# Weight sums built by DMA in DRAM: 128 small steps over all of a layer in place of 64 larger steps inside its attention loop

## The chip, the cores and the metric

The kernel runs on one core of one Trainium2 chip. The metric is the device time of one execution in microseconds. Of the kernel before, three runs gave 1980.7, 1981.05 and 1982.59 us; the median, 1981.05 us, is the figure that the changed kernel is compared with.

## The reference

Two layers of a decoder trunk, for one sequence of 512 tokens and 1024 channels in float32. Cut to what matters here:

```python
for layer in range(2):
    z = rmsnorm(x) @ w_in[layer]                    # one wide projection, split into the mixers' inputs
    # three mixers: conformer convolution, sparse attention, latent attention
    x = x + (g_conv * y_conv + g_attn * y_nsa + g_mla * y_mla) @ w_out[layer]
    x = x + memory_cross_attention(rmsnorm(x), rmsnorm(mem), w_xq, w_xkv, w_xo)
    gate, up = split(rmsnorm(x) @ w_gate_up[layer])  # w_gate_up: 1024 x 5632, gate | up
    x = x + (silu(gate) * up) @ w_down[layer]
return rmsnorm(x)
```

The feed-forward product with `w_gate_up` is done with a scheme that multiplies fewer blocks than the plain product and needs, beside the weights, four sums of weight blocks. With g and u for the gate and up halves and 1 and 2 for the upper and lower 512 rows, the kernel puts together `u1+u2`, `g1+u1+u2`, `g1+u1` and `g1+g2+u1+u2` by signs that it arranges elsewhere; each is 512 rows by 2560 columns.

## The kernel before, in words

Every weight arrives by a load on SP's queue into a tile `raw` of 1 MB (two buffers), is split by `hilo` (L90 to L98) into a high part (ScalarE, L94) and a low remainder (VectorE, L95), and is used in three products per block, `mm3` (L84 to L87). TensorE is the engine with the most work. A layer passes, in order, through: the norm of x and its transposes; the projections with the convolution and the compression work (the loads `in_cmp_w_...` belong to it); the attention loop at the end of `mix`; the products with `w_out` (`residual`); cross attention; its `residual`; the feed-forward with the sums; the `residual` with `w_down`.

The four sums of a layer, `sums[0]` to `sums[3]`, are built in DRAM by DMAs alone: a plain DMA copies a block of weights into a sum, an accumulating DMA adds another block to it, and the last two steps of a job add one sum to another. `summed` (L330) makes a generator of these steps. A job is eight steps on one block of 320 columns and all 512 rows (row pieces of 1280 bytes, 640 KB a step): four copies, then four additions; eight jobs make 64 steps a layer. The attention loop calls `next(paced, None)` once per turn (L1099), which issues one step. Only POOL's queue can issue these steps, in order, and each waits for three things where they apply: the newest product of `mm3` at the time it was written (`latest["product"]`, a semaphore of TensorE, so that steps are paced), the step that wrote the sum it reads or adds to, and the DMA that used its completion semaphore before.

POOL has little else to do, but what it has stands in the same queue: the power -1/2 of every norm (`rs`, L202, in `rstd_of`; `mv`, L772, in the layer norm of the convolution; `rst`, L1032), for which VectorE waits before it can go on, and small memsets (`Pc`, `PTh`, `xt`, `u`). The feed-forward loads the sums column block by column block (two of 256 columns by 512 rows at a time, `ub` and `uc` in the last loop over m).

The order of instructions on each engine is made by a scheduler from the order of the code and its own estimates, so a step written between two products may land a few instructions away.

Of the kernel before, what the change touches and what calls it, by code (L numbers as in the profile page):

```python
# [3 lines left out]

# [9 lines left out]
OP = mybir.AluOpType  # L14
# [15 lines left out]
FFN = 2816  # L30
# [21 lines left out]
def kernel(ctx, tc, x, mem, positions, rel_bias, norm_mix, norm_xattn, norm_mem, norm_ffn, norm_final,  # L52
# [31 lines left out]
    def mm3(o, lh, ll, rh, rl, start, stop):  # L84
        nc.tensor.matmul(o, lh, rh, start=start, stop=False)  # L85
        nc.tensor.matmul(o, lh, rl, start=False, stop=False)  # L86
        latest["product"] = nc.tensor.matmul(o, ll, rh, start=False, stop=stop)  # L87

    latest = {}

    def hilo(hi, lo, src, scale=None):

# [97 lines left out]
    def load_gain(vec):  # L190
        g = new("gB", (128, D))
        nc.scalar.dma_start(g, rows_bcast(vec, D))
        return g
# [136 lines left out]
    def summed(l):  # L330

        W = w_gate_up[l]
        n, step = FFN - 256, 320
        sums = [dr.tile([512, n], F32, name=f"sums{l}_{i}") for i in range(4)]
        quarter = [(0, FFN), (0, 0), (0, 0), (512, 0)]
        jobs = []
        for c in range(0, n, step):
            s = [t[:, c:c + step] for t in sums]  # L340
            w = [[W[r:r + 512, o + 256 + c:o + 256 + c + step] for r in (0, 512)] for o in (0, FFN)]
            jobs.append([(s[0], w[1][0], None), (s[2], w[0][0], None), (s[1], w[0][0], None), (s[3], w[0][1], None),
                         (s[0], w[1][1], OP.add), (s[2], w[1][0], OP.add), (s[1], s[0], OP.add), (s[3], s[1], OP.add)])

        def steps():
            for job in jobs:
                for dst, src, op in job:
                    yield
                    d = nc.gpsimd.dma_start(dst, src, accum_op=op) if op else nc.gpsimd.dma_start(dst, src)  # L349

                    tc.add_manual_dep(d.ins, latest["product"].ins.name, mybir.DependencyInfo(
                        mybir.DependencyClass.Sync, mybir.DependencyReason.DATA), reason="paced")

        return sums, steps()

    def mix(l, x_src, g_mix, x_now, more_x, paced):
        W = w_in[l]


# [732 lines left out]
        for u, (_, mix, args) in enumerate(units):  # L1092
            scores = start(u + 2 if u < 3 else u + 3)
            for now in mix(*args, ready[u]):
                next(scores, None)
                products()
                products = now
                pump(6 if u < 4 else 4 if args[1] > 1 else 3)
                next(paced, None)  # L1099
            for _ in scores:  # L1100
                pump(1)
        products()
# [15 lines left out]
    def residual(acts, kt, w, xs, after, tail=2):  # L1118

        tags = ("t", "t", "s", "s", "mm", "mm", "mm", "pv")  # L1120
        accs = [bank(tag) for tag in tags]
        held = []

        def tokens(a, t):

            if len(a.shape) == 3:
                return a[:, t // 2, t % 2 * 128:(t % 2 + 1) * 128]
            return a[:, t * 128:(t + 1) * 128]

        def run(group, t):  # L1130
            for c in range(2):
                for k, wh, wl in group:
                    xh, xl = (tokens(a, t) for a in acts(k))
                    o = accs[2 * t + c]
                    r = slice(c * 512, (c + 1) * 512)
                    nc.tensor.matmul(o, xh, wh[:, r], start=k == 0, stop=False)  # L1136
                    nc.tensor.matmul(o, xh, wl[:, r], start=False, stop=False)  # L1137
                    nc.tensor.matmul(o, xl, wh[:, r], start=False, stop=k == kt - 1)  # L1138

        for u in row_units(w, kt):  # L1140
            held.append(u)
            if len(held) > tail:
                g = [held.pop(0)]
                for t in range(NT):
                    run(g, t)
        for t in range(NT):
            run(held, t)
            for c in range(2):
                nc.vector.tensor_tensor(xs[t][c], xs[t][c], accs[2 * t + c], op=OP.add)
            after(t)  # L1150
# [12 lines left out]
    x_src = xin  # L1163
    g_mix = load_gain(norm_mix[0])
    xs = load_x(xin, [], (0,))
    for l in range(L):
        sums, paced = summed(l)
        fin = mix(l, x_src, g_mix, lambda t: xs[t], lambda: l or load_x(xin, xs, (1, 2, 3)), paced)
        xs = load_x(x_src, [])


# [121 lines left out]


        last = l == L - 1
        g_next = load_gain(norm_final if last else norm_mix[l + 1])
        act = []
        homes = ["op"] * 10 + ["ca"] * 2 + ["PT"] * 2 + ["gm", "h", "h", "u"] + ["o8"] * 2 + ["BT"] * 2
# [129 lines left out]

        xs = load_x(xd, [])
        if not last:  # L1430
            def after(t):
                for c in range(2):
                    nc.scalar.dma_start(xd[t * 128:(t + 1) * 128, c * 512:(c + 1) * 512], xs[t][c])
        else:
            def after(t):
                for c, h in enumerate(norm_rows(xs[t], g_next)):
                    nc.sync.dma_start(out[0, t * 128:(t + 1) * 128, c * 512:(c + 1) * 512], h)
# [56 lines left out]
```

## Time and profile before

| | |
|---|---|
| runs, us | 1980.7, 1981.05, 1982.59 |
| profiled execution: its own time | 1980.79 us |
| its span (first to last instruction) | 1979.0 us |
| mean granted TensorE clock | 0.991 of 2.4 GHz |
| TensorE busy | 1929.8 us (98%) |
| VectorE, ScalarE, POOL busy | 69%, 50%, 8% |
| DMA moved | 317.92 MB, mean 161 GB/s |
| of it on POOL's queue (the steps, and 16 stores of x) | 88.09 MB, 20.6% of 16 engines' span |

The profiled execution took 1.8 us more than its span, which lies around the first and last instruction. In the page's slices the DMA engines are over 0.8 busy only in two stretches, 134 to 440 us and 1108 to 1425 us of the span: there the 64 steps of a layer are issued. Elsewhere they are at 0.2 to 0.6. A busy TensorE is not one at its peak, since the ends of matmuls are modelled; idle time in front of its instructions is what the waits show.

### The profile page before, as it was taken

How to read it: one execution, taken by the hardware profiler on the slowest of the kernel's cores; microseconds unless marked ns; L12 is line 12 of the kernel's file. 1: busy time of each engine (PE TensorE's matmuls, PEld its weight loads, DVE VectorE, ACT ScalarE, POOL GpSimd, SP SyncE). 2: the span in 40 equal slices, each digit the busy share in tenths (PEclk: the TensorE clock that was granted, in tenths of full speed). 3: DMA queues.
4: the chain of work that ended last, by engine and by line, in shares of the span. 5: the costliest groups of instructions: out<-in, count | busy, mean ns of one | idle time of the engine just before them, and what ended most of it. 6: DMA issues, size and time to landing. Idle time of an engine off the chain costs nothing.

```text
span 1979.0 us, 28842 instructions
## 1 busy us (share of the span) xinstructions
PE 1929.8 (98%) x11136; PEld 1679.1 (85%) x11136; DVE 1373.4 (69%) x2525; ACT 980.3 (50%) x1858; POOL 157.2 (8%) x236
## 2 busy tenths in 40 slices
PE   8998998999999999999999989989999999999998
PEld 8877887888888999988888868868888889999886
DVE  6988898764466877752279889976644677777423
ACT  5366556763355545531254755666633465545312
POOL 0001122210001000000000011222100010000000
PEclk9999999999999999999999989999999999999999
DMA  5247999893432455553232588979933434556431
GB/s 163 72 142 186 236 213 231 207 231 110 148 117 103 153 182 190 171 193 107 93 110 78 168 221 203 227 196 210 229 115 117 139 117 158 184 176 196 161 107 64
DMA packets 241397, 317.92 MB, mean 161 GB/s; under 512 B 12480, under 2 KB 203203, under 8 KB 241260
## 3 DMA queue, kind: packets, MB, share of 16 engines
q1 hardware_dynamic: 194028, 220.83, 34.4%
q0 software_dynamic: 44288, 88.09, 20.6%
q10 hardware_dynamic: 2944, 7.17, 1.0%
q8 instruction: 87, 1.43, 0.3%
q14 instruction: 50, 0.41, 0.1%
HBM read 307.64 MB, written 92.30 MB: 202 GB/s over the span
## 4 chain that ended last, share of the span: by engine, by line
PE 78%; issue 7%; DMA 6%; DVE 5%; ACT 2%; POOL 1%; SPq 0%; DVEq 0%; POOLq 0%; ACTq 0%
PE ps_mm L85 12%; PE ps_mm L86 12%; PE ps_mm L87 12%; PE ps_s L85 2%; PE ps_s L86 2%; PE ps_s L87 2%; PE ps_t L85 2%; PE ps_t L86 2%; PE ps_t L87 2%; PE ps_mm L1136 2%; PE ps_mm L1138 2%; PE ps_mm L1137 2%; DMA raw<-in_cmp_w_v_dram 2%; PE ps_t L952 2%; PE ps_t L1136 1%
## 5 line engine op out<-in xcount | busy, mean ns | idle before, releaser
L95 DVE TENSOR_TENSOR wl<-raw,wh 128x1024 fp32r<-128x1024 f32 (+5 forms) x382 | 451.3, 1185 | 382.9 <-ACT wh L94 381.4
L94 ACT CAST wh<-raw 128x1024 fp32r<-128x1024 f32 (+5 forms) x382 | 387.9, 1019 | 580.1 <-PE ps_pv L1138 206.7
L85 PE MATMUL ps_mm<-hTh,wh 128*128 128x512 f32 (+1 forms) x1152 | 417.5, 363 | 0.5 <-DVE kc L95 0.5
L86 PE MATMUL ps_mm<-hTl,wh 128*128 128x512 f32 (+1 forms) x1152 | 413.0, 359 | 0.0
L87 PE MATMUL ps_mm<-hTh,wl 128*128 128x512 f32 (+1 forms) x1152 | 411.9, 358 | 0.5 <-DVE wl L95 0.5
L87 PEld LDWEIGHTS ps_mm<-hTh,wl 128*128 128x128 f32 x1152 | 218.9, 190 | 33.0 <-DVE wl L95 1.3
L85 PEld LDWEIGHTS ps_mm<-hTh,wh 128*128 128x128 f32 x1152 | 219.4, 191 | 31.1 <-issue 3.3
L86 PEld LDWEIGHTS ps_mm<-hTl,wh 128*128 128x128 f32 x1152 | 219.3, 190 | 26.5 <-issue 0.7
L456 DVE SCALAR_TENSOR_TENSOR ca<-u,vT,ca 128x512 f32<-128x512 f32 x240 | 177.4, 747 | 2.9
L349 POOL DMA_DIRECT2D sums<-in_w_gate_up_dram x96 | 78.4, 824 | 337.2 <-PE ps_mm L87 229.0
L94 ACT CAST PTh<-ps_t 128x512 fp32r<-128x512 f32 (+4 forms) x136 | 70.3, 517 | 67.8 <-PE ps_t L952 53.2
L916 ACT ACTIVATE P<-P,ss 128x512 f32<-128x512 f32 (+3 forms) x128 | 71.3, 558 | 58.9 <-DVE ss L913 58.1
L85 PE MATMUL ps_s<-rh,wh 128*128 128x256 f32 x320 | 90.6, 283 | 0.0
L86 PE MATMUL ps_s<-rl,wh 128*128 128x256 f32 x320 | 90.6, 283 | 0.0
L87 PE MATMUL ps_s<-rh,wl 128*128 128x256 f32 x320 | 90.6, 283 | 0.0
L95 DVE TENSOR_TENSOR PTl<-ps_t,PTh 128x512 fp32r<-128x512 f32 (+2 forms) x120 | 71.6, 597 | 8.6 <-ACT PTh L94 7.5
L924 ACT ACTIVATE P<-P,sr 128x512 f32<-128x512 f32 (+3 forms) x128 | 63.2, 553 | 17.0 <-DVE sr L922 16.8
L202 POOL TENSOR_TENSOR rs<-rs,mhalf 128x1 f32<-128x1 f32 x32 | 22.4, 699 | 600.8 <-DVE rs L199 589.3
L85 PE MATMUL ps_mm<-op,wh 128*128 128x512 f32 (+1 forms) x192 | 69.1, 360 | 0.0
L86 PE MATMUL ps_mm<-op,wh 128*128 128x512 f32 (+1 forms) x192 | 68.2, 355 | 0.0
L87 PE MATMUL ps_mm<-op,wl 128*128 128x512 f32 (+1 forms) x192 | 68.2, 355 | 0.0
L85 PEld LDWEIGHTS ps_s<-rh,wh 128*128 128x128 f32 x320 | 61.4, 192 | 0.0
(552 smaller groups left out, 4553.4 us busy)
## 6 DMA issues: line engine op xcount, KB each, us to landing
sums<-in_w_gate_up_dram POOLq DMA_DIRECT2D x96, 640.0 KB, 7.2
raw<-sums SPq DMA_DIRECT2D x80, 512.0 KB
raw<-in_w_in_dram SPq DMA_DIRECT2D x32, 1024.0 KB
raw<-in_w_gate_up_dram SPq DMA_DIRECT2D x24, 1024.0 KB
raw<-in_w_down_dram SPq DMA_DIRECT2D x22, 1024.0 KB
sums<-sums POOLq DMA_DIRECT2D x32, 640.0 KB, 7.5
raw<-in_w_in_dram SPq DMA_DIRECT2D x26, 512.0 KB
raw<-in_w_gate_up_dram SPq DMA_DIRECT2D x20, 512.0 KB
```

Of the source, the lines that this page charges most:

```text
L85: nc.tensor.matmul(o, lh, rh, start=start, stop=False)
L86: nc.tensor.matmul(o, lh, rl, start=False, stop=False)
L87: latest["product"] = nc.tensor.matmul(o, ll, rh, start=False, stop=stop)
L94: nc.scalar.copy(hi, src)
L95: nc.vector.tensor_tensor(lo, src, f(hi), op=OP.subtract)
L349: d = nc.gpsimd.dma_start(dst, src, accum_op=op) if op else nc.gpsimd.dma_start(dst, src)
L456: nc.vector.scalar_tensor_tensor(c, u[:, j:j + T], cw[:, m, j:j + 1], c, op0=OP.mult, op1=OP.add)
L916: nc.scalar.activation(p[:, c], p[:, c], AF.Exp, bias=s[:, k:k + 1], scale=-1.0, accum_out=s[:, 4 + k:5 + k])
L924: nc.scalar.activation(P[k], P[k], AF.Copy, scale=r[:, k:k + 1])
L952: nc.tensor.transpose(tp[:, w:w + 128], P[k][:, j * 128:(j + 1) * 128], ident)
L1136: nc.tensor.matmul(o, xh, wh[:, r], start=k == 0, stop=False)
L1137: nc.tensor.matmul(o, xh, wl[:, r], start=False, stop=False)
```

## The change

The steps get another shape and another pace; their number of bytes stays.

- A step takes 64 rows by 1280 columns (row pieces of 5120 bytes, 320 KB) in place of 512 rows by 320 columns. A job is still the same eight steps; 8 row groups by 2 column halves make 16 jobs, 128 steps a layer.
- `tick` is called by the third matmul of every `mm3` and of every triple in `residual`, and issues a step at each fifth call in layer 0 and each sixth in layer 1, waiting for the product that called it.
- Layer 0's steps begin with the first products of the kernel and end in the cross attention. Layer 1's begin in layer 0's last `residual` (with `w_down`) and end in layer 1's second `residual`.
- The loop at the end of `mix` no longer issues steps. Order on SP's queue is the same in both kernels; on the other engines neighbours trade places at a few points.

```diff
-        latest["product"] = nc.tensor.matmul(o, ll, rh, start=False, stop=stop)
-
-    latest = {}
+        tick(nc.tensor.matmul(o, ll, rh, start=False, stop=stop))
...
-        n, step = FFN - 256, 320
+        n, rows = FFN - 256, 64
         sums = [dr.tile([512, n], F32, name=f"sums{l}_{i}") for i in range(4)]
...
-        for c in range(0, n, step):
-            s = [t[:, c:c + step] for t in sums]
-            w = [[W[r:r + 512, o + 256 + c:o + 256 + c + step] for r in (0, 512)] for o in (0, FFN)]
-            jobs.append([(s[0], w[1][0], None), (s[2], w[0][0], None), (s[1], w[0][0], None), (s[3], w[0][1], None),
-                         (s[0], w[1][1], OP.add), (s[2], w[1][0], OP.add), (s[1], s[0], OP.add), (s[3], s[1], OP.add)])
...
+            for r, c in pairs(range(0, 512, rows), (0, n // 2)):
+                s = [t[r:r + rows, c:c + n // 2] for t in sums]
+                w = [[W[q + r:q + r + rows, o + 256 + c:o + 256 + c + n // 2] for q in (0, 512)] for o in (0, FFN)]
+                for dst, src in ((s[0], w[1][0]), (s[2], w[0][0]), (s[1], w[0][0]), (s[3], w[0][1])):
+                    yield dst, src, None
+                for dst, src in ((s[0], w[1][1]), (s[2], w[1][0]), (s[1], s[0]), (s[3], s[1])):
+                    yield dst, src, OP.add
...
+    paced = {"count": 0, "every": 1, "steps": iter(())}
+
+    def tick(product):
+        paced["count"] += 1
+        if paced["count"] % paced["every"] == 0:
+            for dst, src, op in islice(paced["steps"], 1):
+                d = nc.gpsimd.dma_start(dst, src, accum_op=op) if op else nc.gpsimd.dma_start(dst, src)
+
+                tc.add_manual_dep(d.ins, product.ins.name, mybir.DependencyInfo(
+                    mybir.DependencyClass.Sync, mybir.DependencyReason.DATA), reason="paced")
...
                 pump(6 if u < 4 else 4 if args[1] > 1 else 3)
-                next(paced, None)
...
-                    nc.tensor.matmul(o, xl, wh[:, r], start=False, stop=k == kt - 1)
+                    tick(nc.tensor.matmul(o, xl, wh[:, r], start=False, stop=k == kt - 1))
...
     xs = load_x(xin, [], (0,))
+    sums, paced["steps"] = summed(0)
+    paced["every"] = 5
...
         xs = load_x(xd, [])
         if not last:
+            sums, paced["steps"] = summed(1)
+            paced["every"] = 6
```

Three places on POOL's queue show what moves. The names in the rows: `sums0_1_148` is `sums[1]` of layer 0 (the last number is a buffer's), `mv` and `rs` are the powers for VectorE, PE and DVE with a number are semaphores of TensorE and VectorE, DMASW with a number is the completion semaphore of an earlier step.

First, POOL in layer 0's layer norm of the convolution, around 310 to 350 us of the span. Before:

```order
L349 DMA sums0_3_150<-in_w_gate_up_dram 512x320 [waits PE_49]
L349 DMA sums0_0_147<-in_w_gate_up_dram 512x320 [waits DMASW0_49,PE_49]
L349 DMA sums0_2_149<-in_w_gate_up_dram 512x320 [waits DMASW5_49,DMASW1_49,PE_49]
L772 TENSOR_TENSOR mv_3262<-mv_3262,mhalf_72 128x1 [waits DVE_49]
L872 MEMSET Pc_3361 128x128 [waits Activation_49]
L349 DMA sums0_1_148<-sums0_0_147 512x320 [waits DMASW4_49,DMASW2_49,PE_49]
L772 TENSOR_TENSOR mv_3325<-mv_3325,mhalf_72 128x1 [waits DVE_49]
L349 DMA sums0_3_150<-sums0_1_148 512x320 [waits DMASW6_49,DMASW7_49,DMASW3_49,PE_49]
L772 TENSOR_TENSOR mv_3388<-mv_3388,mhalf_72 128x1 [waits DVE_49]
L349 DMA sums0_0_147<-in_w_gate_up_dram 512x320 [waits PE_49]
L772 TENSOR_TENSOR mv_3433<-mv_3433,mhalf_72 128x1 [waits DVE_49]
```

After:

```order
L354 DMA sums0_3_150<-in_w_gate_up_dram 64x1280 [waits PE_49]
L775 TENSOR_TENSOR mv_3284<-mv_3284,mhalf_72 128x1 [waits DVE_49]
L875 MEMSET Pc_3382 128x128 [waits Activation_49]
L775 TENSOR_TENSOR mv_3347<-mv_3347,mhalf_72 128x1 [waits DVE_49]
L354 DMA sums0_0_147<-in_w_gate_up_dram 64x1280 [waits DMASW0_49,PE_49]
L775 TENSOR_TENSOR mv_3409<-mv_3409,mhalf_72 128x1 [waits DVE_49]
L354 DMA sums0_2_149<-in_w_gate_up_dram 64x1280 [waits DMASW5_49,DMASW1_49,PE_49]
L775 TENSOR_TENSOR mv_3454<-mv_3454,mhalf_72 128x1 [waits DVE_49]
L354 DMA sums0_1_148<-sums0_0_147 64x1280 [waits DMASW4_49,DMASW2_49,PE_49]
L354 DMA sums0_3_150<-sums0_1_148 64x1280 [waits DMASW6_49,DMASW7_49,DMASW3_49,PE_49]
```

Before, the additions of a sum to a sum, which wait for the landing of the step right ahead of them, stand in front of the second and third `mv`. After, nothing stands between the first two `mv` but a memset, and the steps in front of the third and fourth wait for semaphores of steps that are further back.

Second, POOL at the end of layer 0's `residual` with `w_down` and the start of layer 1, around 975 to 1065 us. Before:

```order
L509 MEMSET xt_10528 128x16x2 [waits DVE_49,PE_49]
L509 MEMSET xt_10528 128x16x2
L202 TENSOR_TENSOR rs_9687<-rs_9687,mhalf_72 128x1 [waits DVE_49]
L202 TENSOR_TENSOR rs_9719<-rs_9719,mhalf_72 128x1 [waits DVE_49]
L202 TENSOR_TENSOR rs_9743<-rs_9743,mhalf_72 128x1 [waits DVE_49]
L202 TENSOR_TENSOR rs_9767<-rs_9767,mhalf_72 128x1 [waits DVE_49]
L1032 TENSOR_TENSOR rst_10361<-rst_10361,mhalf_72 128x8 [waits DVE_49]
L447 MEMSET u_11641 128x30 [waits DVE_49,Pool_49]
```

After:

```order
L354 DMA sums1_2_9062<-in_w_gate_up_dram 64x1280 [waits PE_49]
L512 MEMSET xt_10636 128x16x2 [waits DVE_49,PE_49]
L512 MEMSET xt_10636 128x16x2
L354 DMA sums1_1_9061<-in_w_gate_up_dram 64x1280 [waits PE_49]
L200 TENSOR_TENSOR rs_9780<-rs_9780,mhalf_72 128x1 [waits DVE_49]
L354 DMA sums1_3_9063<-in_w_gate_up_dram 64x1280 [waits PE_49]
L200 TENSOR_TENSOR rs_9812<-rs_9812,mhalf_72 128x1 [waits DVE_49]
L354 DMA sums1_0_9060<-in_w_gate_up_dram 64x1280 [waits DMASW0_49,PE_49]
L200 TENSOR_TENSOR rs_9836<-rs_9836,mhalf_72 128x1 [waits DVE_49]
L200 TENSOR_TENSOR rs_9860<-rs_9860,mhalf_72 128x1 [waits DVE_49]
L354 DMA sums1_2_9062<-in_w_gate_up_dram 64x1280 [waits DMASW5_49,DMASW1_49,PE_49]
```

Before, the four `rs` of layer 1's first norm stand in a row with no step near them. After, each of the first three has a step right in front of it, which waits for a product.

Third, POOL in layer 1's norms after `w_out`, around 1520 to 1540 us. Before:

```order
L202 TENSOR_TENSOR rs_14472<-rs_14472,mhalf_72 128x1 [waits DVE_49]
L202 TENSOR_TENSOR rs_14504<-rs_14504,mhalf_72 128x1 [waits DVE_49]
L202 TENSOR_TENSOR rs_14740<-rs_14740,mhalf_72 128x1 [waits DVE_49]
L202 TENSOR_TENSOR rs_14778<-rs_14778,mhalf_72 128x1 [waits DVE_49]
L202 TENSOR_TENSOR rs_14816<-rs_14816,mhalf_72 128x1 [waits DVE_49,Activation_49]
L202 TENSOR_TENSOR rs_14854<-rs_14854,mhalf_72 128x1 [waits DVE_49]
```

After:

```order
L354 DMA sums1_0_9060<-in_w_gate_up_dram 64x1280 [waits PE_49]
L354 DMA sums1_2_9062<-in_w_gate_up_dram 64x1280 [waits PE_49]
L200 TENSOR_TENSOR rs_14861<-rs_14861,mhalf_72 128x1 [waits DVE_49]
L200 TENSOR_TENSOR rs_14900<-rs_14900,mhalf_72 128x1 [waits DVE_49]
L354 DMA sums1_1_9061<-in_w_gate_up_dram 64x1280 [waits PE_49]
L354 DMA sums1_3_9063<-in_w_gate_up_dram 64x1280 [waits PE_49]
L200 TENSOR_TENSOR rs_14939<-rs_14939,mhalf_72 128x1 [waits DVE_49,Activation_49]
L354 DMA sums1_0_9060<-in_w_gate_up_dram 64x1280 [waits DMASW0_49,PE_49]
L200 TENSOR_TENSOR rs_14977<-rs_14977,mhalf_72 128x1 [waits DVE_49]
L354 DMA sums1_2_9062<-in_w_gate_up_dram 64x1280 [waits DMASW5_49,DMASW1_49,PE_49]
```

Before, the steps have ended here. After, five of them stand in front of or between the last four `rs`.

## Rows read from the trace of the kernel before

**Rows 1.** The page, busy time of the engines, share of the span

```profile
PE 1929.8 (98%) x11136; PEld 1679.1 (85%) x11136; DVE 1373.4 (69%) x2525; ACT 980.3 (50%) x1858; POOL 157.2 (8%) x236
```

**Rows 2.** Stretches: us, busy by engine, clock, DMA share, GB/s

```profile
39.00:134.00 95.00, 94.24 (x452) 76.50 (x451) 85.66 (x174) 47.78 (x84) 2.28 (x3) 1.00 0.32 97
134.00:440.00 306.00, 293.36 (x1557) 243.67 (x1556) 252.24 (x596) 190.69 (x414) 58.05 (x81) 0.99 0.90 218
876.00:1108.00 232.00, 230.27 (x1096) 192.74 (x1095) 129.91 (x232) 85.29 (x153) 6.52 (x13) 1.00 0.33 104
1108.00:1425.00 317.00, 302.40 (x1587) 250.44 (x1586) 256.66 (x601) 194.53 (x422) 58.23 (x82) 0.98 0.87 213
```

**Rows 3.** The same view, fifty us inside layer 0's mixers

```profile
350.00:400.00 50.00, 50.00 (x272) 42.45 (x271) 36.17 (x81) 34.84 (x67) 9.87 (x14) 1.00 0.95 218
```

**Rows 4.** Waits of PE, whole span: us in total, times, longest

```profile
PE ps_mm L566 <- ACT w L94: 7.4, 4, 3.2
PE ps_mm L766 <- DVE m L883: 7.1, 2, 3.9
...
PE ps_pv L939 <- ACT P L924: 2.5, 2, 1.3
PE ps_pv L963 <- DVE PTl L95: 2.5, 2, 1.7
```

**Rows 5.** Chain that ended last, 300 to 345: start us, us, what

```profile
316.59 7.94 DMA sums<-in_w_gate_up_dram
...
325.05 7.79 DMA sums<-sums
...
333.43 1.05 POOL sums L349
334.48 0.60 POOL mv L772
...
344.25 0.23 PE ps_mm L85
```

**Rows 6.** Waits of DVE, whole span, columns as in rows 4

```profile
DVE hn L215 <- POOL rs L202: 11.7, 19, 1.4
...
DVE cn L774 <- POOL mv L772: 9.7, 6, 2.3
...
DVE Pc L875 <- DMA BT<-vd: 3.0, 2, 1.9
```

**Rows 7.** Timeline of DVE near 327: start, us, operation, idle before it

```profile
326.87 0.81 DVE L774 TENSOR_SCALAR cn<-ps_mm,mv 128x512 f32<-128x512 f32 x1 [0.52 <-POOL mv L772]
```

**Rows 8.** Stretch after the gap at 1314, columns as in rows 2

```profile
1313.80:1317.20 3.40, 3.15 (x10) 2.51 (x11) 2.94 (x11) 0.81 (x2) 0.00 (x0) 0.50 1.18 233
```

**Rows 9.** Chain that ended last, weight loads, both layers

```profile
178.16 8.52 DMA raw<-in_cmp_w_v_dram
...
1108.36 6.27 DMA raw<-in_w_in_dram
...
1127.20 8.50 DMA raw<-in_cmp_w_v_dram
...
1153.91 9.20 DMA raw<-in_cmp_w_v_dram
```

**Rows 10.** POOL's DMA queue in 178.2:181.2, 138:139.5, 188.5:190.5: packets, MB, share

```profile
q0 software_dynamic: 447, 0.55, 116.5%
...
q0 software_dynamic: 113, 0.58, 92.3%
...
q0 software_dynamic: 306, 0.39, 116.4%
```

**Rows 11.** Operations on sums: ns min/median/max, landing us; one issue row

```profile
L349 POOL DMA_DIRECT2D sums<-in_w_gate_up_dram x96: 623/678/1092, 133.9 to 1404.8; - x96
...
DMA to landing us min/median/max: 4.3/7.3/11.9
...
xd<-x POOLq DMA_DIRECT2D x16, 256.0 KB, 2.3
```

More of the change, by code (lines that the diff above doesn't have):

```diff
@@ L2 @@
 from contextlib import ExitStack
-from itertools import chain, cycle, islice
+from itertools import chain, cycle, islice, product as pairs
 import concourse.bass as bass
@@ L334, in summed, with mix @@
         W = w_gate_up[l]
-        n, step = FFN - 256, 320
+        n, rows = FFN - 256, 64
         sums = [dr.tile([512, n], F32, name=f"sums{l}_{i}") for i in range(4)]
-        quarter = [(0, FFN), (0, 0), (0, 0), (512, 0)]
-        jobs = []
-        for c in range(0, n, step):
-            s = [t[:, c:c + step] for t in sums]
-            w = [[W[r:r + 512, o + 256 + c:o + 256 + c + step] for r in (0, 512)] for o in (0, FFN)]
-            jobs.append([(s[0], w[1][0], None), (s[2], w[0][0], None), (s[1], w[0][0], None), (s[3], w[0][1], None),
-                         (s[0], w[1][1], OP.add), (s[2], w[1][0], OP.add), (s[1], s[0], OP.add), (s[3], s[1], OP.add)])
-        def steps():
[L346 to L352, printed above, removed]
-        return sums, steps()
-    def mix(l, x_src, g_mix, x_now, more_x, paced):
+        def steps():
+            for r, c in pairs(range(0, 512, rows), (0, n // 2)):
[5 more added lines that the diff above has]
+                    yield dst, src, OP.add
+        return sums, steps()
+    paced = {"count": 0, "every": 1, "steps": iter(())}
[6 more added lines that the diff above has]
+                    mybir.DependencyClass.Sync, mybir.DependencyReason.DATA), reason="paced")
+    def mix(l, x_src, g_mix, x_now, more_x):
         W = w_in[l]
@@ L1165 @@
     xs = load_x(xin, [], (0,))
+    sums, paced["steps"] = summed(0)
+    paced["every"] = 5
     for l in range(L):
-        sums, paced = summed(l)
-        fin = mix(l, x_src, g_mix, lambda t: xs[t], lambda: l or load_x(xin, xs, (1, 2, 3)), paced)
+        fin = mix(l, x_src, g_mix, lambda t: xs[t], lambda: l or load_x(xin, xs, (1, 2, 3)))
         xs = load_x(x_src, [])
@@ L1295 @@
         last = l == L - 1
+        assert not list(paced["steps"])
         g_next = load_gain(norm_final if last else norm_mix[l + 1])
@@ L1430 @@
         if not last:
+            sums, paced["steps"] = summed(1)
+            paced["every"] = 6
+        if not last:
             def after(t):
```

## Prediction

> **What bounds the kernel now.** I read the page's busy times first. TensorE is busy 98% of the span [rows 1], so a change to DMAs can only give back what TensorE loses in gaps and at its lower clock. Then busy time by stretch, which says where that is. In the two stretches in which the steps are issued, 134 to 440 and 1108 to 1425 us, TensorE idles 306.0 - 293.4 = 12.6 and 317.0 - 302.4 = 14.6 us; in the quiet ones before them, 39 to 134 and 876 to 1108, it idles 0.8 and 1.7 us [rows 2]. The DMA share is 0.90 and 0.87 in the first pair, 0.32 and 0.33 in the second. But full DMA engines alone do not stop TensorE: inside the attention loop, 350 to 400, they stand at 0.95 and TensorE is busy all of 50.00 us [rows 3]. So the loss hangs on certain waits, and the third view, what TensorE waits for, names them [rows 4]. Two kinds matter.
>
> The first is the layer norm of the convolution. PE L766, L939 and L963 wait 7.1 + 2.5 + 2.5 = 12.1 us, all of it at about 326 to 336 and 1302 to 1314 us. The chain of waits shows why [rows 5]: an addition lands in 7.94 us, the next step, which reads that sum, lands in 7.79, the step behind it issues for 1.05, and only then can POOL do the `mv` that VectorE waits for. VectorE's own waits agree: 9.7 us in six waits for `mv`, 3.0 us in two for the load of `BT` [rows 6].
>
> The second is a load of compression weights, for which PE L566 waits 7.4 us in four waits [rows 4]. On the chain such loads take 8.52, 8.50 and 9.20 us, and a load of the same 1 MB that starts just before layer 1's first step takes 6.27 [rows 9]. In the three us after the issue at 178.16, POOL's queue alone had 116.5% of 16 engines, since packets overlap [rows 10]; the load had to stand behind additions.
>
> Behind such gaps TensorE runs at the lower of its two levels: after the gap at 1314 the granted clock is 0.50, which is 1.2 of 2.4 GHz, for 3.4 us, and 1.7 us of work are lost [rows 8]. There are four more such stretches near these waits, three of 3.4 us and one of 6.8.
>
> **The change, part by part.** 1. *The work of the steps.* A packet of a copy carries 0.58 MB / 113 = 5.1 KB in 0.923 x 1.5 us x 16 / 113 = 196 ns; one of an addition carries 1.28 KB in 1.164 x 2.0 x 16 / 306 = 122 ns [rows 10]. So a copy of 640 KB costs 1.6 us of all 16 engines, an addition 3.9, and a layer's 32 + 32 steps 175 us of the 306. The new copies have 64 rows of the same 5120 bytes: 0.8 us each, 50 us for 64. An addition of 5120-byte rows is not in the trace. At the rate of the present additions it takes four packets' time, 1.95 us a step, 125 us a layer; at the rate of a copy 0.8 us, 50 us. I take 1.95, since it is the same operation; then the work stays 175 us, and at best it is 100. Layer 0 spreads it over 39 to some 595 us: 31% on top of the 0.3 that the loads need, and in the mixers 0.6 in place of 0.9. Nothing of this is on the path by itself.
>
> 2. *The layer norm.* In the first order excerpt the additions whose predecessor is one step back are gone from in front of the second and third `mv`; what stands there now waits for a product that TensorE passes before and for landings four or more steps old. A wait of VectorE for an `mv` that found POOL free is 0.52 us [rows 7]. So of 9.7 us six floors, 3.1, stay and 6.6 go. With 3.0 for `BT`, which comes over less crowded engines, 9.6. The first `mv` of layer 0 still stands behind a copy's issue of some 0.65 us [rows 11], so 8.9. What is late next is VectorE itself, 257 us busy of 317 there [rows 2]; so I give TensorE 7.5 of the 12.1 us, between 3 (that VectorE fills in most) and 12.1. With the 1.7 us of low clock at 1314: **-9.2**.
>
> 3. *The loads.* With at most one step of 0.8 to 1.95 us ahead of or inside it, the floor of 6.27 becomes about 7.0. At 178.16 that gives 1.5, at 1153.91 2.2, at 1127.20 1.5, of which I count half, since VectorE works beside it. The load at 1108.36 loses 0.7, since it now meets steps from the start. Sum 3.75. Bounds: 0, if the sprinkled steps hit every load as they do now, and the 7.4 us of L566. The four other stretches of low clock cost 17.0 / 2 = 8.5 us; I count a fifth: **-5.4** together.
>
> 4. *New ground.* Steps now run from 39 to 134, 440 to 595, 876 to 1108 and 1425 to 1545 us. TensorE has next to no idle time there, and DMA goes from about 0.35 to 0.65, less than where TensorE stays full today [rows 3]. Nothing shows a cost; but loads there land later. From 0 to +10 (five loads late by 2 us each); I take **+2**.
>
> 5. *POOL's queue.* Twice as many issues of 0.65 to 1.05 us take POOL's time, which is free (8% busy). What they can hold up are 18 powers of norms that had no step near them or are now among steps. Second and third order excerpt: the steps in front wait for a product that TensorE has passed when the norm's sum of squares is ready, so a power meets at worst an issue in progress. VectorE waits 11.7 us for 19 such powers now, 0.6 each [rows 6]. If a quarter of the 18 wait 0.8 us more, 3.6 us of VectorE, of which TensorE, with products to do beside the norms, loses **+1**. Bounds 0 and +8, the latter if landings hold the queue.
>
> A rule that speaks against the change: the Trainium skill, "DMA: Bandwidth & Descriptors", Anatomy of one DMA, gives a DMA on this path about 2 us fixed and its bytes over 436 GB/s, and its Rules for kernel authors say to merge transfers. By that, as an estimate, 64 landings of 3.5 us become 128 of 2.75 us, 224 us becoming 352 a layer, of which a queue that waits for landings would see the more. Here the measurement is far above it: 640 KB lands in 4.3 to 11.9 us, median 7.3, and 256 KB of x in 2.3 [rows 11]. So the rule stands in no term, and the second rival is priced from the rows.
>
> Sum: -9.2 - 5.4 + 2 + 1 = -11.6 on the profiled execution's 1980.8 us (span 1979.0 and 1.8 around it) = 1969.2; against the median of 1981.05, 0.26 more, it is **1969 us**.
>
> **The rivals.** *No change, 1981 us.* VectorE is 81 to 82% busy over both step stretches [rows 2] and fills what POOL sets free, and every load still meets a step. For it: TensorE idles 0 us at a DMA share of 0.95 [rows 3]. Against it: two additions in a row, 16 us, stand in the chain [rows 5], and the order takes them from the `mv`. It needs terms 2 and 3 to shrink to about -3 in all.
>
> *Slower, 1989 us: POOL held by landings.* A product block of 15 matmuls of 0.23 us [rows 5], five triples, lasts 3.4 us, so in dense stretches a step is written every 3.4 us in layer 0 and 4.1 in layer 1. The last step of a job reads what the one before it wrote. If 320 KB lands in 2.3 us, as 256 KB of x do, nobody waits; if it needs 7.3, as 640 KB do [rows 11], POOL stands 3 to 4 us longer at each job's end, and falls behind the pace by that. Then every power of a norm behind it is late: eight of the 18 late by some 2.5 us with no products beside gives +20, against -11.6: 1989. It decides from a landing of about 4 us in dense stretches up, if the queue does not catch up before a norm; a job's other six waits are older, which speaks against it.
>
> *More, 1952 us.* If TensorE gets back all of 12.1 and 7.4 us and the low clock's 1.7 + 8.5, it is 29.7 less, without terms 4 and 5 1951. Against it: L566 stands behind ScalarE and VectorE too, and the latter has 18% to spare.
>
> That the change does not do what it says (steps bunched by the scheduler) I rule out: the order shows them one by one between other work.
>
> **How the numbers follow.** Forecast 0.55 (some 1961 to 1976), more 0.10, no change 0.20, slower 0.15. A measurement of this kernel can tell about 0.2%, 4 us: under 1977 is faster, over 1985 slower. From the cases: faster 0.65, same 0.20, slower 0.15. The range runs from 1955, into the larger gain, to 1983, over the case of no change and into the slower one; outside are about 0.08 below and 0.12 above.
>
> **What would show it.** Right: the waits of VectorE for `mv` under 5 us, PE L766 under 3; the chain without `sums` steps; loads of compression weights at 6.3 to 7.5 us; DMA share 0.55 to 0.7 from 39 to 595; idle time of TensorE from 134 to 440 down to 6 or 8 us, and fewer stretches at 0.50. Wrong: POOL waiting for the landing of a sum in front of an `rs`, VectorE waiting much more than 11.7 us for `rs` (term 5); new waits of ScalarE for `raw` in the quiet stretches (term 4); additions of some 490 ns a packet would confirm 1.95 us, 200 ns the lower bound.

## The result, and the profile after

The changed kernel takes 1956.39 us (median of four runs, 1953.59 to 1958.55) against 1980.88 for the kernel before (median of four): ratio 0.9875, 95% interval 0.9858 to 0.9892. That is 24.5 us faster; the forecast was 11.6. The direction and the range held, the size did not. Experiment 15 ran the changed kernel again: 0.9873 (0.9860 to 0.9887).

The profiled execution has a span of 1953.5 us, 25.5 less than before. First the page's busy times, which answer to [rows 1]:

```profile
PE 1919.8 (98%) x11136; PEld 1674.0 (86%) x11136; DVE 1371.1 (70%) x2525; ACT 979.3 (50%) x1858; POOL 218.7 (11%) x364
```

Then the four stretches of [rows 2] (us, busy by engine, clock, DMA share, GB/s):

```profile
39.00:134.00 95.00, 92.56 (x441) 74.84 (x440) 83.51 (x172) 47.09 (x84) 18.67 (x27) 1.00 0.69 176
134.00:440.00 306.00, 302.67 (x1614) 252.07 (x1614) 261.05 (x611) 198.54 (x431) 45.51 (x79) 1.00 0.58 151
876.00:1108.00 232.00, 230.20 (x1111) 193.35 (x1111) 136.42 (x245) 89.48 (x163) 38.81 (x63) 1.00 0.66 171
1108.00:1425.00 317.00, 313.41 (x1642) 260.62 (x1641) 261.59 (x604) 198.14 (x425) 40.67 (x71) 0.99 0.54 142
```

TensorE now idles 3.3 us from 134 to 440 (12.6 before) and 3.6 from 1108 to 1425 (14.6). In the stretches that took over steps it idles 2.4 (0.8) and 1.8 us (1.7). VectorE is busy 261 us of 306 (252 before) and keeps up. (The stretches are cut at the same us in both spans, so those of the changed kernel hold a little more work: 1614 matmuls against 1557 from 134 to 440.)

Both traces hold 11136 matmuls, so the start of the nth in one can be set against the nth in the other, and the change of that difference says where time went. This is the main reading of the case:

| place (us of before) | changed by, us | forecast |
|---|---|---|
| loads of compression weights, 142 to 191 | -7.2 | |
| the same in layer 1, 1117 to 1171 | -8.6 | both -5.4 |
| layer norm of the convolution, 316 to 362 | -5.6 | |
| the same in layer 1, 1300 to 1346 | -7.6 | both -9.2 |
| a weight load at 105 | +2.0 | |
| norms and loads behind `w_out`, 540 to 600 | +0.5 | |
| norm in front of the feed-forward, 634 | +3.7 | all new ground and POOL +3 |
| elsewhere, small pieces | -2.9 | |
| sum | -25.7 | -11.6 |

Of the small pieces, 1.0 us is a stretch at the lower clock at 870 that the trace before has and this one has not, and 1.2 us come back at 1520 to 1550, on new ground. In the trace of experiment 15 the loads have -15.2 in both layers together (-15.8 here) and the layer norms -13.2 (-13.2 here), so the places are the same and the sizes agree within 0.6 us.

The waits of TensorE, with the lines of [rows 4] under their new numbers (L766 is now L769, L566 is L569, L939 is L942; total, times, longest):

```profile
PE ps_t L220 <- DVE hn L213: 6.6, 3, 2.9
...
PE ps_mm L769 <- DVE m L886: 0.7, 1, 0.7
...
PE ps_mm L569 <- ACT w L92: 0.5, 1, 0.5
PE ps_pv L942 <- ACT P L927: 0.4, 1, 0.4
```

Of 7.4 us at the compression weights 0.5 is left, of 12.1 at the layer norm 1.1 (L963 waits no more). A third wait went with the loads, one that [rows 4] leaves out: a product of the attention waits for `PTh`, which ScalarE casts only when it is through with the work behind a late compression load. Before:

```profile
PE ps_pv L750 <- ACT PTh L94: 3.0, 2, 1.6
```

After, under its new numbers, 0.2 us in one wait is left:

```profile
PE ps_pv L753 <- ACT PTh L92: 0.2, 1, 0.2
```

What now leads the list is L220, the transposes of a norm. VectorE's waits, as in [rows 6]:

```profile
DVE hn L213 <- POOL rs L200: 12.8, 18, 2.3
...
DVE cn L777 <- POOL mv L775: 1.2, 2, 0.7
```

The wait for `mv` fell from 9.7 us in six to 1.2 in two: four of the six floors of 0.52 us that I left standing are gone too. The wait for the other norms' `rs` is 12.8 us, 11.7 before. Behind the loads it is ScalarE that waits directly; its row before:

```profile
ACT w L94 <- DMA raw<-in_cmp_w_v_dram: 11.3, 4, 4.0
```

and after:

```profile
ACT w L92 <- DMA raw<-in_cmp_w_k_dram: 2.3, 1, 2.3
...
ACT w L92 <- DMA raw<-in_cmp_w_v_dram: 0.4, 1, 0.4
```

The chain of waits, for [rows 9]: no landing of a sum stands in the mixers (one issue of 0.77 us does, at 1276) and no `in_cmp_w_v` load stands in it at all. Of the loads that do, those of `in_w_in` take 5.4 to 6.5 us there and one of `in_cmp_w_k` 7.4. The slow loads, 10.1 and 13.0 us long, are on new ground, and there landings of sums stand in the chain too:

```profile
96.60 10.13 DMA raw<-in_w_in_dram
129.49 7.37 DMA raw<-in_cmp_w_k_dram
165.34 6.54 DMA raw<-in_w_in_dram
531.79 5.36 DMA sums<-sums
537.74 0.82 POOL sums L354
...
551.88 12.96 DMA raw<-in_w_xq_dram
...
1083.57 5.63 DMA raw<-in_w_in_dram
...
1100.22 5.38 DMA raw<-in_w_in_dram
```

So two of the prediction's signs of being wrong did show, and cost little. At 537 POOL waits for the landing of a sum in front of an `rs` (term 5). And ScalarE waits for new loads on new ground (term 4), most of all for those of the cross attention; before and after:

```profile
ACT wh L94 <- DMA raw<-in_w_xq_dram: 3.7, 3, 1.9
...
ACT wh L92 <- DMA raw<-in_w_xq_dram: 18.6, 4, 8.7
```

TensorE loses 0.5 us net there, as the table has it.

Of five stretches at 1.2 GHz in the mixers before (20.5 us, [rows 8] is one) one of 3.4 us is left, and there is a new one behind the gap at 626; at this level they lose at most 1.7 us each:

```profile
1135.00:1138.40 3.40, 3.40 (x10) 2.63 (x9) 3.17 (x9) 2.27 (x6) 0.77 (x1) 0.50 0.00 0
626.40:629.80 3.40, 3.40 (x12) 2.88 (x11) 3.24 (x7) 2.83 (x7) 1.15 (x2) 0.50 0.28 116
```

POOL waits for landings as long as before, but elsewhere. Before:

```profile
POOL sums L349 <- DMA sums<-sums: 62.2, 8, 11.4
POOL sums L349 <- DMA sums<-in_w_gate_up_dram: 23.4, 5, 5.9
```

After, 85.0 us against 85.6, for the queue's order of a job is the same (experiment 10 changes it, and these waits go):

```profile
POOL sums L354 <- DMA sums<-sums: 64.8, 13, 8.1
POOL sums L354 <- DMA sums<-in_w_gate_up_dram: 20.2, 5, 4.6
```

### The profile page after: what moved, and what is told of

It is laid out like the page before. It is cut to its first block, busy times and chain, and to the rows that moved or that the text cites. A ratio compares the mean times of both kernels' runs of the same rounds, so it can differ in the third digit from the quotient of the medians.

```text
span 1953.5 us, 29051 instructions
## 1 busy us (share of the span) xinstructions
PE 1919.8 (98%) x11136; PEld 1674.0 (86%) x11136; DVE 1371.1 (70%) x2525; ACT 979.3 (50%) x1858; POOL 218.7 (11%) x364
## 3 DMA queue, kind: packets, MB, share of 16 engines
q0 software_dynamic: 21760, 88.10, 21.2%
## 4 chain that ended last, share of the span: by engine, by line
PE 79%; DVE 6%; DMA 5%; issue 5%; ACT 3%; POOL 1%; SPq 0%; DVEq 0%; POOLq 0%; ACTq 0%
PE ps_mm L85 12%; PE ps_mm L87 12%; PE ps_mm L86 12%; PE ps_t L85 2%; PE ps_t L86 2%; PE ps_t L87 2%; PE ps_s L85 2%; PE ps_s L86 2%; PE ps_s L87 2%; PE ps_mm L1138 2%; PE ps_mm L1139 2%; PE ps_mm L1140 2%; PE ps_t L955 2%; DMA raw<-in_w_in_dram 2%; PE ps_t L1138 2%
## 5 line engine op out<-in xcount | busy, mean ns | idle before, releaser
L354 POOL DMA_DIRECT2D sums<-in_w_gate_up_dram x192 | 119.3, 623 | 877.7 <-PE ps_mm L87 477.2
L354 POOL DMA_DIRECT2D sums<-sums x64 | 49.9, 780 | 285.4 <-PE ps_mm L87 137.7
```

## The experiments

Each kernel was timed in five rounds beside the kernel before; the ratio to it is given with its 95% interval. Theory A says that two waits hold the time, the power of the layer norm behind landings on POOL's queue and the compression loads behind steps, and that both go when steps are spread. The rivals are the row's form and the mere share of busy DMA engines.

**1. New shape, old place.**

```
-        n, step = FFN - 256, 320          # jobs of 512 rows x 320 columns
+        n, rows = FFN - 256, 64           # jobs of 64 rows x 1280 columns
                 next(paced, None)
+                next(paced, None)
```

> The new shape (128 steps of 64 rows of 5 KB) at the old place: two steps at each turn of the attention loop. Theory A (two waits: the layer norm's power held behind landings on POOL's queue, and compression loads behind queued additions): the same bytes go at the same place, only a step lands in about half the time, so the layer norm gets back perhaps half of 13 us and the loads little: about 1974 us, between 1968 and 1980. Rival B (the row length is what pays, 402 ns for 5 KB of addition against four times 121): most of the change's 24 us, 1960 us or less. Rival C (only a lower share of busy DMA engines pays): no change, 1980, as the bytes stay in 306 us.

Measured: 1.0016 (1.0003 to 1.0029). The new shape alone gives nothing. By the matmul starts (of the slowest of its twelve runs, 1992.4 us against a median of 1986.2) the layer norms gain 2.9 and 5.4 us and the loads nothing, but new waits come at 426 and 1406 us (+5.7, +6.9) and the late store of 634 us, below, is there too (+3.7). POOL has twice the issues in the same 306 us, and its memsets of `Pc` come late. A wait of TensorE, and under it one of VectorE:

```profile
PE ps_pv L962 <- DVE PTl L95: 7.0, 3, 4.2
```

VectorE, waiting for POOL's memset:

```profile
DVE Pc L874 <- POOL Pc L871: 15.3, 5, 6.2
```

**2. Old shape, new pace.** Steps of 512 rows of 1280 bytes at each tenth and twelfth product.

```
-    paced["every"] = 5
+    paced["every"] = 10
...
-            paced["every"] = 6
+            paced["every"] = 12
```

> The old shape (64 steps of 512 rows of 1280 bytes) at the new pace: one at each tenth product in layer 0, each twelfth in layer 1, from the first products on. Theory A: a load meets one addition at most and no two dependent additions stand in front of the layer norm's powers, so most of the 16 us of the loads and of the 13 us of the layer norm comes back, less some since a step is twice as long: about 1960 us, between 1956 and 1966. Rival B (row length): 1977 to 1981. Rival C (DMA share): 1957, as the share falls just as far.

Measured: 0.9915 (0.9899 to 0.9931), some 17 of the 25 us. The pace carries the change. By itself this run does not tell theory A from the rival of the share, since the share falls as well. What is missing against the changed kernel lies mostly in layer 0's mixers: the loads give back 3.2 us there (7.2 in the changed kernel) and the layer norm 3.0 (5.6). New ground takes +3.1 at the load of 105 us (2.0), and a wait at 1178 takes +3.0; the late store of 634 us, on the other hand, is not there.

**3. The kernel before without the power in the layer norm.**

```
-            nc.gpsimd.tensor_tensor(mv[:, 3:4], mv[:, 2:3], mhalf[:, 0:1], op=OP.pow)
-            nc.vector.tensor_scalar(c, tp, mv[:, 0:1], mv[:, 3:4], ...
+            nc.vector.tensor_scalar(c, tp, mv[:, 0:1], mv[:, 2:3], ...
```

> The kernel before without the power -1/2 of the convolution's layer norm: VectorE uses the variance itself, so nothing of that norm stands on POOL's queue (this part of the computation is changed); steps as before. Theory A: the two jumps of the layer norm, 5.7 us in layer 0 and 7.7 in layer 1, come back and nothing else does: about 1967.5 us, between 1965 and 1971. A rival (the layer norm waits for its load of BT, which the crowded DMA engines hold up, and POOL is only late beside it): at most 3 to 5 us, 1976 to 1978.

Measured: 0.9960 (0.9944 to 0.9975), 8 us. The trace, of one of its two slowest runs, has only 2.1 of them. In it layer 1's norm gains 5.4 us and layer 0's nothing (+0.4): 1.3 us are won at 326 and lost again from 332 to 339, where the clock is at its lower level. The rival holds in part. With the power gone, the load of `BT`, for which VectorE waited 3.0 us, becomes the wait, and TensorE waits at L962 instead. VectorE's row:

```profile
DVE Pc L874 <- DMA BT<-vd: 8.7, 2, 5.4
```

and TensorE's:

```profile
PE ps_pv L962 <- DVE PTl L95: 4.7, 2, 3.2
```

So the layer norm had two late things, one behind the other; experiment 6 shows that both come from the steps.

**4. The kernel before, steps begun 14 turns later.**

```
+                turn += 1
-                next(paced, None)
+                for _ in range(0 if turn <= 14 else 2 if turn > 48 else 1):
+                    next(paced, None)
```

> The kernel before with its first step 14 turns later (after the compression loads, at about 195 us of the span), made up by two steps a turn after turn 48, behind the layer norm. Theory A: loads of 6.3 us and no low clock in 138 to 191 and 1117 to 1171, 7.5 + 8.6 us back, and the layer norm's 13 us stay lost: about 1965 us, between 1961 and 1970; where two steps a turn delay later loads, up to 1972. The rival (loads are bound by VectorE and ScalarE beside them, as I had priced): 4 to 5 us, 1976.

Measured: 1.0302 (1.0287 to 1.0317), 60 us slower, and yet the clearest run. Up to the last compression load it does what theory A says: -8.5 us in layer 0 from 142 to 191, -8.8 in layer 1. Where the steps then stand it loses 5.8 us at the layer norm and 7.4, 9.0 and 18.3 behind it in layer 0, 2.3, 17.8 and 18.3 in layer 1. ScalarE's wait for the loads is nearly gone:

```profile
ACT w L94 <- DMA raw<-in_cmp_w_v_dram: 0.5, 2, 0.3
```

VectorE's waits for POOL are not:

```profile
DVE Pc L875 <- POOL Pc L872: 66.2, 4, 19.8
DVE cn L774 <- POOL mv L772: 17.4, 4, 8.5
```

The chain in front of one of the late memsets shows why (start us, us, what): two steps from the weights and one from sum to sum land, 25.8 us in all, before POOL can go on.

```profile
420.84 17.03 DMA sums<-in_w_gate_up_dram x2
...
438.37 8.76 DMA sums<-sums
...
450.96 0.22 POOL Pc L872
```

This is the prediction's slower rival, POOL held by landings. It is real; it needs more steps in the attention loop, not the ones of the change.

**5. No steps at all.** `sums` are plain blocks of `w_gate_up`.

```
-        return sums, steps()
+        return sums, iter(())             # and sums[i] = a block of W
```

> No step at all: the feed-forward loads plain blocks of weights in the place of the four sums (the sums are left out of the computation); loads, order and products as in the changed kernel. It gives the floor of any shape and pace. If the losses that the two traces place at loads, layer norm and the changed kernel's new gaps (2.0 us at 105, 1.1 at 547, 3.7 at 634) are all that steps cost: about 1949 us, between 1945 and 1953. If spread steps still slow TensorE everywhere a little (contention that no wait shows): 1940 or less.

Measured: 0.9828 (0.9814 to 0.9841), 1948 us: the forecast floor. So steps cost the kernel before 34 us by the runs, and the changed kernel keeps some 9 of them. The trace is of the slowest of the five runs (1954.1) and has 27 us, all of it at the places of the table: -5.8 and -9.0 at the loads, -4.7 and -7.5 at the layer norms. Between them the starts of its matmuls keep their distance to those of the kernel before, but for +0.7 us at 850 to 890 and -0.5 at 1840 to 1870, so no cost is spread over TensorE where no wait shows; where the other 7 us of the runs lie, this trace does not tell. It has 6.8 us at 1.2 GHz in layer 0's loads, with no step and no late load near (columns as in [rows 2]):

```profile
167.29:174.11 6.82, 6.52 (x18) 5.27 (x19) 4.72 (x13) 3.98 (x10) 0.00 (x0) 0.50 0.03 11
```

TensorE had just waited for VectorE, 1.04 and 0.67 us, as it does in the changed kernel, whose clock stayed up. So the 1.4 us by which layer 0's loads gain more in the changed kernel than without any step are not owed to the steps.

**6. The kernel before, no step around the layer norm.** By its count of turns the last addition of a layer is left out as well.

```
+                for _ in range(0 if 33 <= turn <= 43 else 2 if turn in range(47, 66, 3) else 1):
+                    next(paced, None)
```

> The kernel before with no step in turns 33 to 43, around the layer norm of the convolution, seven of them made up by second steps at turns 47 to 65. Theory A, with what the kernel without the power taught (there a load of branch weights took the place of the power in layer 0): with neither steps in front of the power nor steps around that load, both layers get their layer norm back, 5.7 + 7.7 us, and the seven doubled turns cost a part of it: 1970 us, between 1966 and 1976. The rival (the layer norm is bound by VectorE or by loads that were queued long before): 1980 or more.

Measured: 1.0115 (1.0102 to 1.0129). The layer norm gets back 4.6 and 7.5 us, 12.1 in all, so [rows 5] were read rightly. But seven doubled turns cost 8.5 + 9.6 us in layer 0 and 7.9 + 8.8 in layer 1. The first of each pair stands behind a load that lands late; ScalarE's wait for that of layer 0, 385 to 412 us:

```profile
ACT wh L94 <- DMA raw<-in_w_in_dram: 7.4, 1, 7.4
```

The second stands behind a power: POOL waits for two landings in a row before it can do an `rs` of the next norm, for which VectorE waits up to 12.7 us (1.4 before, [rows 6]). The chain in layer 1, and VectorE's waits:

```profile
1432.00 18.83 DMA sums<-in_w_gate_up_dram x2
...
1452.34 0.61 POOL rs L202
...
DVE hn L215 <- POOL rs L202: 34.8, 19, 12.7
```

TensorE's waits over the whole span show both, the power's first:

```profile
PE ps_mm L87 <- DVE wl L95: 14.5, 3, 7.1
PE ps_pv L962 <- ACT PTh L94: 10.7, 2, 5.5
```

Together, 4 and 6 return 17.3 + 12.1 us = 29.4, near what the table above has for these places (-29.0), and both show that the attention loop had no room: what is moved inside it is paid for there.

**7 and 8. Row and size apart, at the new pace.** 128 rows of 5 KB (640 KB, each tenth and twelfth product), and 256 rows of 1280 bytes (320 KB, each fifth and sixth).

```
-        n, rows = FFN - 256, 64
+        n, rows = FFN - 256, 128          # 7
+        n, rows, step = FFN - 256, 256, 320   # 8
```

> The new pace with steps of 128 rows of 5 KB, 640 KB, one at each tenth or twelfth product: the old step's size with the new row. The kernel with the old shape at this pace stood at 0.9915, the changed one at 0.9875. If the small step makes the difference (a load meets half as much, a landing is sooner): 1964 us, as with the old shape. If the long row does (402 ns of addition for 5 KB against four times 121): 1957.

> The new pace of one step at each fifth or sixth product with steps of 256 rows of 1280 bytes, 320 KB: the new step's size with the old row. If the small step makes the difference: 1957 us. If the long row does: 1964. If each does half: both this and the kernel of 128 long rows at 1960.

Measured: 0.9892 (0.9878 to 0.9905) and 0.9873 (0.9859 to 0.9886). With experiment 2 and the changed kernel this is a square:

| | rows of 1280 bytes | rows of 5120 bytes |
|---|---|---|
| 640 KB a step | 0.9915 | 0.9892 |
| 320 KB a step | 0.9873 | 0.9875 |

At 640 KB the long row is worth some 0.2%, at 320 KB nothing; the small step is worth 0.4% with short rows and 0.2% with long ones. Of these only the 0.4% is clear of the intervals. The Trainium skill, "DMA: Bandwidth & Descriptors", Rules for kernel authors, says to coalesce many small transfers into a large one. The pair with short rows goes the other way, at sizes above the 64 KB that the page names. A reason that fits, though no run isolates it: what the kernel waits for is not the steps' own bandwidth but the load that stands behind a step.

**9 to 12. Can the rest be had?** Stores of x behind the cross attention on ScalarE's queue (9), two jobs in turn so that a step stands at least four behind the one it needs (10), both (11), both with layer 0's steps from 110 us on at each fourth product (12).

```
-                nc.gpsimd.dma_start(xd[t * 128:(t + 1) * 128, ...], xs[t][c])
+                nc.scalar.dma_start(xd[t * 128:(t + 1) * 128, ...], xs[t][c])    # 9
...
+                for two in zip(*jobs):                                           # 10
+                    yield from two
```

> The changed kernel (ratio 0.9875 to before) with the stores of x behind the cross attention of layer 0 issued by ScalarE instead of POOL, so that no store stands in front of the feed-forward norm's powers. If the 3.7 us at 623 to 631 us come from the late first store on POOL's queue (3.2 us behind the x that it waits for, in both kernels of 128 steps, in none of 64): 0.9857, 1953 us on the scale of before 1981. The rival (POOL itself wakes late there, whatever comes first): 0.9875, and the power itself is late.

> The changed kernel with the steps of two jobs in turn, ordered so that a step stands at least four behind the one whose sum it needs (one or two behind before): POOL's 85 us of waiting for landings should be nearly gone. If POOL held by landings costs time only at the powers at 535 to 549 us: 1.1 to 1.6 us less, ratio 0.9868, 1955 us. If such waits also set back the pace elsewhere: up to 5 us less.

> Both edits, stores on ScalarE and jobs two by two: if they add up, 0.985, 1951 us, within 3 us of the kernel without steps (0.9828); if the store's edit does nothing, as with jobs two by two alone.

> Both edits, and layer 0's steps begin after 80 products (at about 110 us, behind the load that took 10.1 us at 96.6) and come at each fourth product. If that load is late for the steps: 2 us less than with both edits, 0.984, 1949 us. If the denser pace brings the loads at 134 to 190 late again: 2 to 5 us more, 0.986 to 0.988.

Measured: 0.9915, 0.9857 (0.9843 to 0.9871), 0.9908, 0.9934. Layer 0 gets nothing from stores on ScalarE (4.1 us are lost at 634, 3.7 in the changed kernel), and layer 1, which was never late, loses 8 us at 1500 to 1600. There the stores' issues stand among ScalarE's own squares for the norms, which may hold these back; that is not shown apart. TensorE's row:

```profile
PE ps_t L220 <- DVE hn L213: 10.6, 7, 2.6
```

Two jobs in turn take POOL's 85.0 us of landing waits to none, and the time moves by no more than the intervals overlap: in the changed kernel those waits stand where nobody waits for POOL. A faster pace of layer 0 (12) costs some 8 us at 554 us against 11; the 2 us at 105 come back there, but in 10 and 11 too, so the later start is not what brings them. Nor are they won: all three lose 1.8 to 2.5 us at 138 to 155 instead, where the changed kernel gains 0.6.

**13. The kernel before, copies in the place of additions.** Same turns, same bytes; the sums are left out.

```
-                    d = nc.gpsimd.dma_start(dst, src, accum_op=op) if op else ...
+                    d = nc.gpsimd.dma_start(dst, src)
```

> The kernel before with plain copies in the place of its 32 additions a layer (the sums are left out of the computation), at the same turns, of the same bytes: 64 x 1.6 = 102 us of 16 engines a layer instead of 175. If loads and layer norm were late because the steps all but fill the DMA engines in the attention loop (share 0.9, a queue that never empties): loads and norm come back at the old place too, about 1956 us, between 1950 and 1962. If it is the place alone (any step ahead of a load or a power makes it late): 1972 or more.

Measured: 0.9947 (0.9935 to 0.9960), 10.5 us, between both. The DMA share falls to 0.68 (columns as in [rows 2]):

```profile
134.00:440.00 306.00, 293.96 (x1558) 244.03 (x1557) 252.50 (x596) 191.20 (x414) 45.67 (x82) 0.99 0.68 221
```

and ScalarE's wait for the loads from 11.3 to 6.3 us:

```profile
ACT w L94 <- DMA raw<-in_cmp_w_v_dram: 6.3, 4, 3.0
```

Layer 1 gains 4.5 us at its last compression load and 5.7 at its layer norm and loses 1.7 at 1178; layer 0 gains 0.4 in all its mixers. Some 1.7 us more are a stretch at the lower clock at 1850, far from any step, that this trace has not. So the slow additions are a third to two fifths of what the change gains, with the fuller engines and with POOL's waits for a sum's landing, which fall from 62.2 to 25.8 us here; these are not told apart. The rest goes only when steps are moved away (experiments 2, 4 and 6).

**14 to 16. On one chip:** 256 short rows with two jobs in turn, the changed kernel, 128 rows of 2560 bytes with two jobs in turn.

> The changed kernel's pace with steps of 256 rows of 1280 bytes, two jobs in turn: the two edits that stood at 0.9873 and 0.9857 alone, without the late store at 623 us. If they add up: 0.984, 1950 us, near the kernel without steps (0.9828). If they do not: 0.987, as the changed kernel.

> The changed kernel once more, on the same chip as the others here, for a direct comparison: 0.9875, and its first store of x behind the cross attention 3.2 us late again. If that lateness was chance, its trace is without it.

> As the kernel of 256 short rows two jobs in turn, with steps of 128 rows of 2560 bytes (320 KB as well): if size and order set the time and the row length does not, the same time within 2 us; if steps of 64 rows alone make the store late, it is not late here.

Measured: 0.9895 (0.9881 to 0.9908), 0.9873, 0.9885 (0.9869 to 0.9901). The edits do not add up. None of these versions beats the changed kernel beyond its interval; the places where some time is lost shift with each of them, by 1 to 4 us.

## Why the prediction was right and wrong

*What bounds the kernel: right, but for one wait.* The waits of [rows 4] held the time, and with them L750's, behind the same loads: 29.0 us come back at their places (27.0 without any step, experiment 5), and 3.3 net are lost again elsewhere.

*Term 1, the work of steps: right in sum, by chance of two errors.* An addition of 5120 bytes takes some 0.41 us where additions have the engines almost alone, not 0.49 (below). But packets that share the engines with loads take longer: the 16384 packets of 5120 bytes, half of them copies, take 0.39 us in the mean over the whole trace, where 0.196 and 0.41 would make 0.30. All steps and stores on POOL's queue together take 21.2% of the engines' span, 20.6% before (packets, MB, share):

```profile
q0 software_dynamic: 21760, 88.10, 21.2%
```

*Term 2, the layer norm, -9.2: measured -13.2.* The step that failed is "so I give TensorE 7.5 of the 12.1 us", for a VectorE that would be late next. It was not: TensorE got 11.0 of 12.1, and experiment 6 got 12.1 back with nothing but the steps' absence. The load of `BT` was rightly counted with it; experiment 3 shows that with the power alone gone layer 0 gains nothing.

*Term 3, the loads, -5.4: measured -15.8.* This is the term that was mis-sized most. It had 3.75 for late loads and 1.7 for the low clock. By the matmul starts the late loads gave back 11.0 and the clock 4.8.

The 3.75 priced each load by its length on the chain above 7.0 us. That failed at every load: 2.4 us came back behind the one at 178.16 (priced at 1.5), 3.4 behind 1153.91 (2.2), some 2.5 behind 1127.20 (half of 1.5), 0.9 behind 1108.36 (which was to lose 0.7), and 1.9 in layer 0 behind loads that have no price at all. What showed the size were the waits. TensorE got back 6.9 of L566's 7.4, which was only the bound, and 2.8 of L750's 3.0, which stood in no term: a late load holds ScalarE, and with it what ScalarE has to do next. I read the load from the chain, but not ScalarE's own wait for it, 11.3 us, now 2.7 for loads of compression weights, and 0.5 for `in_cmp_w_v` in experiment 4, with no step near.

"I count a fifth" of the low clock behind the gaps failed as well: of the four stretches' 17 us at 1.2 GHz 3.4 are left. What came back inside them is 1.4, 1.5, 0.3 and 1.6 us; in that of 6.8 us TensorE also stood idle for 1.1, and the 3.4 that are left stand there. Not all of it is earned: the 1.4 us at 170 are lost in experiment 5 too, where no step is.

*Terms 4 and 5, +3: measured +3.3, net of small gains.* Right in size by luck, not in place. The load at 96.6 us, 10.13 us long, costs 2.0. At 540 us POOL, held by the landing of a sum in front of a power, makes VectorE wait 1.5 us; a power was to meet "at worst an issue in progress". Experiment 10 takes 1.6 us away there, but loses 1.5 more than the changed kernel right behind it, at 575 to 590. The 3.7 at 634 stand behind a late store, in no term. And 2.9 of gains elsewhere, 1.0 of it the clock's at 870, hide as much loss.

*The rivals.* "More", 1952 us, was nearest; the argument against it, VectorE and ScalarE behind L566, was the wrong one. Its own sum is not what happened either: the clock gave less than its 10.2 us, and L750, which it left out, made up for part. "No change" leaned on [rows 3], 50.00 us at a share of 0.95, and this row misled: experiments 4 and 6 show that a few more steps in that loop cost 7 to 18 us at a time. A full stage without a gap does not show how much slack is left in it. Loads were issued in those 50 us too, and ScalarE waited 0.8 us for one; why TensorE never did, no run shows. "Slower" needs twice the steps of that loop.

## What to carry to other kernels

When background DMAs fill a stage, price a load from the wait of the engine that reads it, with the other work that this engine then does late, and book the low clock right behind the gap with it, as a bound: here it came back in part. Moving such DMAs inside a full stage only moves the wait; moving them out of it pays. Which step size is best there these runs show for short rows alone: 320 KB beat 640 by 0.4%. An in-order queue that holds both DMAs and small results is late only where someone waits for the small results: look there, not at its sum of waits.

## What the runs showed of the hardware

An addition of 5120-byte rows costs less per byte than one of 1280. In 92.9 to 94.9 us of the changed kernel additions had the engines almost alone; POOL's queue there (packets, MB, share):

```profile
q0 software_dynamic: 97, 0.41, 102.2%
```

That is 0.41 MB / 5120 = 80 packets in 1.022 x 2.0 us x 16, 0.41 us each, against 4 x 0.122 us for the same bytes [rows 10]. A copy of such a row takes 0.196.

Not expected, and not explained: the first store of x behind layer 0's cross attention starts 3.9 us after the addition that makes x begins, in all three kernels whose steps have 64 rows and whose stores are POOL's (the changed kernel in both its traces, experiments 1 and 10), and 1.0 us after it in those of 128, 256 or 512 rows (before, 2, 7, 8, 14, 16). In the changed kernel's timeline (start, us, operation, idle before it), POOL:

```profile
622.66 1.68 POOL L1292 DMA_DIRECT2D xd<-x  x3 [34.91 <-DVE x L1151]
```

and VectorE:

```profile
618.75 1.28 DVE L1151 TENSOR_TENSOR x<-x,ps_t 128x512 f32<-128x512 f32 x2
```

In experiment 8, POOL:

```profile
624.45 1.16 POOL L1292 DMA_DIRECT2D xd<-x  x2 [32.52 <-DVE x L1151]
```

and VectorE:

```profile
623.47 1.28 DVE L1151 TENSOR_TENSOR x<-x,ps_t 128x512 f32<-128x512 f32 x2
```

The order and the waits on POOL are the same there. It is worth 3.7 us with the low clock behind it: the matmul starts lose 3.6 to 3.7 us at 634 in each kernel with the late store, and nothing in experiments 2, 7, 8, 14 and 16. Why it is late stays open.
